# Attention scores of two layers as three float32r products of split queries and keys

## The chip, the cores and the metric

The kernel runs on one core of a Trainium2 chip. The metric is the device time of one execution in microseconds; the median of several runs is compared. A profiled execution is the source of every row below. TensorE is called PE, its weight loads PEld, VectorE DVE, ScalarE ACT, GpSimd POOL, and SyncE SP.

## What is computed

The reference is a network of three blocks over 512 positions of 1024 channels: one block with stick-breaking attention and an MLP, and then two layers of a second type. The change touches the attention of the second type only, which the reference writes so (cut):

```python
c_kv = _rmsnorm(p[..., o1:o2], g_kv[l])                  # 256 channels
kv = (c_kv @ w_ukv[l]).reshape(b, s, 8, 64 + 64)         # k_nope and v of 8 heads
k_rope = _apply_rope(p[..., o2:o3], cos, sin)            # 32 channels, shared by the heads
sc = q_nope . k_nope + q_rope . k_rope                   # 512 x 512 a head
p = softmax(sc / sqrt(96)); o = p @ v
```

Beside it, in the same layer, a depthwise convolution of 31 taps over 512 channels and a layer norm are computed; both results go into the output projection `w_o`.

## The kernel before, in words

All activations lie with channels on the 128 partitions and the 512 positions along the free dimension. Every big product is made of three float32r products: a tile is split into a high half (`whi`, `xh`, ...: the value cast to float32r) and a low half (the rest), and `mm3` (L505) adds high x high, high x low and low x high into one PSUM bank (L507, L508, L509). Weights are loaded by SP, cast by ACT (L421) and their low halves subtracted on POOL (L422), up to three units ahead of their use.

`layer2` runs once for each of the two layers. In it come, in the order of the code: four tiles of gated units (`glu`); the shared rotary key `pk` (L1165 to L1178); the key/value input, two tiles, and the query input, three tiles (`low_rank`, L1184), each split as soon as it is made, so the key/value input is split without its norm's factor; that factor, `rkv`, is computed inside the first query tile's products (L1210) and the query's factor inside the gate projection that follows (L1213). Since the key/value input is unscaled, the value tiles `v` are multiplied by a column of the factor (`col`, made by `column`, L675, with eight tiny products a layer), and the keys by its row (L1310).

The attention goes over four pairs of heads (L1306). For each pair: one projection makes the keys of both heads, the query projection of each head goes to a PSUM bank of the name `mm`, and DVE multiplies it into the tile `q` (L1315). `attend` (L1271) makes for each of four blocks of queries one score product of float32 tiles (L1275), which is two records of PE in the profile; then DVE's row maximum (L1277), ACT's Exp, and the scaling by the sum's reciprocal, on POOL for the first block and on ACT for the others (L1283). The probabilities are transposed on PE (L1292), split by ACT and DVE (`ph`, `pl`), and multiplied by `v` into the bank `av`. PE works between these on the projections of the next heads and on the output projection (`y_part`).

The convolution's taps fill the other engines: those of DVE are one instruction (L1347), those of POOL an ACT product `pd` and a POOL sum `cacc` (L1361, L1363), four `pd` buffers in turn. A list, `pace`, says behind which ACT instruction each `pd` is issued. The order on each engine is otherwise set by the framework's scheduler when the program is built.

Of the kernel before, what the change touches and what calls it, by code (L numbers as in the profile page):

```python
# [13 lines left out]
F32 = mybir.dt.float32  # L14
FR = mybir.dt.float32r
I32 = mybir.dt.int32
AF = mybir.ActivationFunctionType
ALU = mybir.AluOpType
# [3 lines left out]
P = 128  # L22
S = 512
# [42 lines left out]
PACE_GLU, PACE_ROPE, PACE_RANK, PACE_HEAD = 4, 1, 2, 2  # L66
# [223 lines left out]
class Kern:  # L290
# [274 lines left out]
            ready = cs  # L565


    def split(self, pool, src, tags, scale=None, lo_eng=None):

        hi, lo = (pool.tile([P, S], FR, name=t) for t in tags)  # L570
        self.split_into(hi, lo, src, scale, lo_eng)
        return hi, lo

# [543 lines left out]
    def layer2(self, l, carry=None):  # L1117
        tc, nc = self.tc, self.nc
        mm = nc.tensor.matmul
        V, A, G = nc.vector, nc.scalar, nc.gpsimd  # L1120
# [6 lines left out]
        pp = pa_.__enter__()  # L1127
# [14 lines left out]
        lp = lp_.__enter__()  # L1142
# [3 lines left out]
        pace = []  # L1146

        def glu(pa, pg):
            V.tensor_tensor(out=pg, in0=pg, in1=r, op=ALU.mult)
            V.tensor_tensor(out=pa, in0=pa, in1=r, op=ALU.mult)  # L1150
            u = lp.tile([P, S], F32, name="u", bufs=NCV)
            sig = self.act(AF.Sigmoid, out=u, in_=pg)
            if us:
                pace.extend([sig] * PACE_GLU)
            V.tensor_tensor(out=u, in0=u, in1=pa, op=ALU.mult)
            us.append(u)
# [8 lines left out]
        pk = self.proj(pp, "b", acts)  # L1165
        tkr = lp.tile([P, S], F32, name="tmp", bufs=3)
# [3 lines left out]
        kt = {}  # L1170
        for b in range(2):
            for e in range(2):
                kt[e, b] = lp.tile([P, S], F32, name=f"k{e}{b}")
            if b == 0:
                V.tensor_tensor(out=kt[1, b][0:64], in0=pk[0:64], in1=tkr[0:64], op=ALU.add)
            else:
                A.copy(out=kt[1, b][0:64], in_=kt[1, 0][0:64])
            A.copy(out=kt[0, b][64:128], in_=kt[1, 0][0:64])  # L1178


        r2 = lp.tile([P, S], F32, name="tmp", bufs=3)
        A.activation(out=r2, in_=r, func=AF.Square)

        def low_rank(n, gname, tag, between=None):  # L1184
            out = []
            acc = self.new_acc()
            part = pp.tile([P, S], F32, name="b")
            for j in range(n):
                ps = self.proj(pp, "b", acts, between if j == 0 else None)
                if j == 0:  # L1190
                    A.activation(out=part, in_=ps, func=AF.Square)
                else:
                    V.tensor_tensor(out=part if j < n - 1 else acc, in0=part, in1=self.square(ps), op=ALU.add)
                out.append(self.split(lp, ps, (f"{tag}h{j}", f"{tag}l{j}"), scale=self.v(gname, l, j)))
                pace.extend([self.last_hi] * PACE_RANK)
            return out, acc

        def low_rank_scale(acc, n, dst=None):

            tot, _ = self.total(pp, "b", acc)  # L1200
            w = self.new_acc()
            V.tensor_tensor(out=tot, in0=tot, in1=r2, op=ALU.mult)
            self.rsqrt(w, tot, n * P, tot)
            dst = tot if dst is None else dst
            V.tensor_tensor(out=dst, in0=tot, in1=r, op=ALU.mult)
            return dst

        ckv, acckv = low_rank(2, "g_kv_2", "kv")
        rkv = lp.tile([P, S], F32, name="rho")
        cq, accq = low_rank(3, "g_q_2", "cq", lambda: low_rank_scale(acckv, 2, rkv))  # L1210
        rhos = []

        def q_norm():  # L1213
            rhos.append(self.column(lp, pp, "b", rkv))
            rhos.append(low_rank_scale(accq, 3))

        for i in range(GLU_EARLY, 4):
# [1 line left out]
            self.proj(pp, "b", acts, q_norm if i == GLU_EARLY else None, pa)  # L1219
            self.proj(pp, "b", acts, None, pg)  # L1220
            glu(pa, pg)
        col, rq = rhos
        tq = []
        for e in range(2):
            x = lp.tile([P, S], F32, name=f"tq{e}")
# [15 lines left out]
        def bank(name):  # L1241
            turns[name].rotate(-1)
            return turns[name][0].tile([P, S], F32, name=name)
# [16 lines left out]
        for t in range(4):  # L1260
                vt = lp.tile([P, H2, P], FR, name="v", bufs=4)
                src = vps[t].rearrange("p (h d) -> p h d", d=64)
                A.activation(out=vt[:, :, 0:64], in_=src, func=AF.Identity, scale=col[:, t : t + 1], bias=0.0)
                ins = V.scalar_tensor_tensor(out=vt[:, :, 64:P], in0=src, scalar=col[:, t : t + 1], in1=vt[:, :, 0:64].bitcast(F32), op0=ALU.mult, op1=ALU.subtract)
                vst.append(vt)
        gate.append(ins)

# [3 lines left out]
        def attend(h, q, k, y):  # L1271
            probs = []
            for qb in range(4):
                s = bank("s")
                mm(s, lhsT=q[:, qb * P : (qb + 1) * P], rhs=k, start=True, stop=True)  # L1275
                nm = lp.tile([P, 1], F32, name="nm", bufs=4)
                V.tensor_reduce(out=nm, in_=s, axis=AX.X, op=ALU.max, negate=True)  # L1277
                pr = yp.tile([P, S], F32, name="ul" if h % 2 else "uh")
                sm = lp.tile([P, 1], F32, name="sm", bufs=4)
                ins = self.act(AF.Exp, out=pr, in_=s, bias=nm, accum_out=sm)  # L1280
                V.reciprocal(out=sm, in_=sm)
                if qb >= POOL_BLOCKS:
                    A.activation(out=pr, in_=pr, func=AF.Identity, scale=sm, bias=0.0)  # L1283
                else:
                    G.tensor_tensor(out=pr, in0=pr, in1=sm.broadcast_to((P, S)), op=ALU.mult)
                probs.append(pr)
            pace.extend([ins] * PACE_HEAD + [None] * POOL_TAPS)
            av = bank("av")
            for t in range(4):
                pt = bank("t")  # L1290
                for qb in range(4):
                    nc.tensor.transpose(pt[:, qb * P : (qb + 1) * P], probs[qb][:, t * P : (t + 1) * P], self.ident)  # L1292
                ph = lp.tile([P, S], FR, name="ph", bufs=2)
                pl = lp.tile([P, S], FR, name="pl", bufs=2)
                A.copy(out=ph, in_=pt)
                V.tensor_tensor(out=pl, in0=pt, in1=ph.bitcast(F32), op=ALU.subtract)
                mm(av, lhsT=vst[t][:, h, :], rhs=ph, start=t == 0, stop=False)
                mm(av, lhsT=vst[t][:, h, :], rhs=pl, start=False, stop=t == 3)
            e = h % 2
            me, other = slice(64 * e, 64 * e + 64), slice(64 - 64 * e, 128 - 64 * e)  # L1300
            t = lp.tile([P, S], F32, name="tmp", bufs=3)
            A.copy(out=t[me], in_=av[other])
            V.tensor_tensor(out=y[me], in0=av[me], in1=t[me], op=ALU.add)

        yacts = []
        for p in range(4):  # L1306
            pk = self.proj(pmm, "mm", ckv)
            for e in range(2):
                me = slice(64 * e, 64 * e + 64)
                V.tensor_tensor(out=kt[e, p % 2][me], in0=pk[me], in1=rkv[me], op=ALU.mult)  # L1310
            y = lp.tile([P, S], F32, name="tmp", bufs=3)
            for e in range(2):
                pq = self.proj(pmm, "mm", cq)
                q = lp.tile([P, S], F32, name="q", bufs=2)
                ins = V.tensor_tensor(out=q, in0=pq, in1=tq[e], op=ALU.mult)  # L1315
                gate.append(ins)
                attend(2 * p + e, q, kt[e, p % 2], y)
            yacts.append(self.split(yp, y, ("yh", "yl")))

        ypss = [pmm.tile([P, S], F32, name="mm") for _ in range(2)]  # L1320
# [83 lines left out]
        for i in range(KT):  # L1404
            ps = ypss[i] if i < NYB else self.proj(pmm, "mm", yacts + uacts)
# [7 lines left out]
        pp = pp_.__enter__()  # L1413
# [46 lines left out]
        with tc.manual_schedule(engines={mybir.EngineType.PE}):  # L1460
            for c, ks in enumerate(chunks2()):
# [70 lines left out]
                for m in range(KT - tail):  # L1532
                    ps = ds[m] if m < NDOWN else self.proj(pp, "b", a)
# [140 lines left out]
```

## Time and profile before

| | us |
|---|---|
| median of 3 runs | 1873.52 (1872.75 to 1874.34) |
| profiled execution, whole | 1875.88 |
| its span, first to last instruction | 1874.2 |
| PE busy in the span | 1821.1 |
| DVE, ACT, POOL busy | 1020.8, 1041.2, 1128.6 |

The profiled execution's own time is 1.68 us longer than its span and 2.36 us longer than the median. Busy time says that an engine has something in work; two instructions of PE overlap, so the step from start to start tells their price, not the duration.

### The profile page before, as it was taken

Reading aid. Unit: us, or ns where it says so; the run is one execution under the profiler, and the core shown is the slowest. Engines: PE = TensorE matmul, PEld = TensorE weight load, DVE = VectorE, ACT = ScalarE, POOL = GpSimd, SP = SyncE. Lnnn points to the kernel's source line nnn. Section 1 sums busy time; section 2 is a strip of 40 time slices with the busy share of each in tenths; the row PEclk is TensorE's granted clock in tenths of the full one; section 3 lists DMA queues with packets and bytes.
Section 4 is the critical chain, followed back from the end, with each engine's and each line's share of the span. In section 5 each row is a group of like instructions: output and inputs, shape, how many; then the busy total and the mean of one; then the engine's idle time right before and its main releaser. Section 6 shows DMA issues by size and latency. Waiting matters only on the chain. (4 is left out here: it accounts for less than half of the span.)

```text
span 1874.2 us, 25701 instructions
## 1 busy us (share of the span) xinstructions
PE 1821.1 (97%) x9726; PEld 1530.7 (82%) x9726; DVE 1020.8 (54%) x1524; ACT 1041.2 (56%) x1630; POOL 1128.6 (60%) x618
## 2 busy tenths in 40 slices
PE   8999999999999999999998999999999998999997
PEld 6877888888888888766778998998866788898996
DVE  5665553725022017898596252553899498253454
ACT  6666643633233236788556373663779566364563
POOL 5233454654554556866577695875866467585872
PEclk9999999999999999999998999999999999999999
DMA  5113386276987852300346595862210214353551
GB/s 188 68 57 107 136 229 199 95 220 177 288 220 223 239 160 79 100 30 23 141 124 214 163 296 168 253 178 83 89 60 23 105 59 136 114 190 135 162 165 45
DMA packets 96092, 268.95 MB, mean 144 GB/s; under 512 B 9824, under 2 KB 11872, under 8 KB 95328
## 3 DMA queue, kind: packets, MB, share of 16 engines
q1 hardware_dynamic: 73376, 188.66, 29.6%
q0 software_dynamic: 19072, 37.75, 11.4%
q10 hardware_dynamic: 3520, 40.90, 5.7%
q8 instruction: 76, 1.25, 0.3%
q14 instruction: 48, 0.39, 0.1%
HBM read 265.18 MB, written 77.59 MB: 183 GB/s over the span
## 5 line engine op out<-in xcount | busy, mean ns | idle before, releaser
L422 POOL TENSOR_TENSOR wlo<-raw,whi 128x1024 fp32r<-128x1024 f32 (+1 forms) x354 | 857.1, 2436 | 609.4 <-ACT whi L421 559.9
L421 ACT CAST whi<-raw 128x1024 fp32r<-128x1024 f32 (+1 forms) x356 | 369.8, 1041 | 470.9 <-PE b L508 343.6
L507 PE MATMUL b<-xh,whi 128*128 128x512 f32 (+1 forms) x720 | 274.1, 381 | 2.7 <-ACT xh L580 2.7
L508 PE MATMUL b<-xl,whi 128*128 128x512 f32 (+1 forms) x720 | 270.4, 376 | 3.5 <-DVE xl L581 3.5
L509 PE MATMUL b<-xh,wlo 128*128 128x512 f32 (+1 forms) x720 | 269.7, 375 | 0.0
L507 PE MATMUL b<-ah,whi 128*128 128x512 f32 (+1 forms) x640 | 242.7, 379 | 0.0
L509 PE MATMUL b<-ah,wlo 128*128 128x512 f32 (+1 forms) x640 | 242.3, 379 | 0.0
L508 PE MATMUL b<-al,whi 128*128 128x512 f32 (+1 forms) x640 | 242.3, 379 | 0.0
L508 PEld LDWEIGHTS b<-xl,whi 128*128 128x128 f32 x720 | 136.2, 189 | 32.4 <-DVE xl L581 4.5
L507 PEld LDWEIGHTS b<-xh,whi 128*128 128x128 f32 x720 | 136.3, 189 | 30.9 <-ACT xh L580 3.1
L509 PEld LDWEIGHTS b<-xh,wlo 128*128 128x128 f32 x720 | 136.2, 189 | 26.1
L509 PEld LDWEIGHTS b<-ah,wlo 128*128 128x128 f32 x640 | 120.4, 188 | 22.3
L507 PEld LDWEIGHTS b<-ah,whi 128*128 128x128 f32 x640 | 120.4, 188 | 22.0
L508 PEld LDWEIGHTS b<-al,whi 128*128 128x128 f32 x640 | 120.4, 188 | 22.0
L1363 POOL TENSOR_TENSOR cacc<-cacc,pd 128x510 f32<-128x510 f32 (+14 forms) x94 | 119.6, 1273 | 26.6 <-ACT pd L1361 22.9
L1347 DVE SCALAR_TENSOR_TENSOR cv<-u,vec,cv 128x497 f32<-128x497 f32 (+13 forms) x146 | 108.2, 741 | 8.5 <-ACT cv L1337 6.6
L1480 DVE TENSOR_TENSOR b<-b,snap 128x256 f32<-128x256 f32 x108 | 46.3, 429 | 83.6 <-PE b L509 82.5
L1534 DVE TENSOR_TENSOR x<-x,b 128x512 f32<-128x512 f32 x46 | 31.5, 688 | 103.6 <-PE b L509 103.6
L1006 DVE TENSOR_TENSOR b<-rl,b 128x512 f32<-128x512 f32 x32 | 22.1, 696 | 96.9 <-ACT rl L1005 96.9
L507 PE MATMUL mm<-xh,whi 128*128 128x512 f32 x176 | 70.8, 402 | 0.0
L508 PE MATMUL mm<-xl,whi 128*128 128x512 f32 x176 | 70.2, 399 | 0.0
L509 PE MATMUL mm<-xh,wlo 128*128 128x512 f32 x176 | 70.1, 398 | 0.0
(502 smaller groups left out, 4434.3 us busy)
## 6 DMA issues: line engine op xcount, KB each, us to landing
raw<-w SPq DMA_DIRECT2D x215, 512.0 KB, 3.6
raw<-S SPq DMA_DIRECT2D x144, 256.0 KB, 2.9
S<-wq POOLq DMA_DIRECT2D x32, 1024.0 KB, 13.0
raw<-wq SPq DMA_DIRECT2D x108, 256.0 KB, 2.9
raw<-w SPq DMA_DIRECT2D x23, 256.0 KB, 2.9
S<-wq POOLq DMA_DIRECT2D x8, 512.0 KB, 8.6
x<-xT SPq DMA_DIRECT2D x8, 256.0 KB, 6.3
S<-wq ACTq DMA_DIRECT2D x4, 512.0 KB, 4.6
```

The source lines that it names most:

```text
L421: cast = nc.scalar.copy(out=hi[:, cs], in_=raw[:, cs])
L422: rest = (eng or nc.gpsimd).tensor_tensor(out=lo[:, cs], in0=raw[:, cs], in1=hi[:, cs].bitcast(F32), op=ALU.subtract)
L507: mm(ps, lhsT=wb[0], rhs=xb[0], start=start, stop=False, **kw)
L508: mm(ps, lhsT=wb[0], rhs=xb[1], start=False, stop=False, **kw)
L509: mm(ps, lhsT=wb[1], rhs=xb[0], start=False, stop=stop, **kw)
L1006: V.tensor_tensor(out=ps, in0=rl, in1=ps, op=ALU.mult)
L1347: ins = V.scalar_tensor_tensor(out=acc[:, o], in0=us[i][:, u], scalar=self.v("w_dw_conv_2", l, i * CONV_K + k), in1=acc[:, o], op0=ALU.mul ...
L1363: G.tensor_tensor(out=acc[:, o], in0=acc[:, o], in1=pd, op=ALU.add)
L1480: V.tensor_tensor(out=out, in0=a, in1=b, op=ALU.add)
L1534: V.tensor_tensor(out=self.x[m], in0=self.x[m], in1=ps, op=ALU.add)
```

## The change

The scores become three float32r products. For that, the query tile is split: ACT casts its high half, POOL subtracts the low half. The keys are split too: ACT casts the projection's rows into a high tile, DVE subtracts the low one (in place of the multiplication by the factor's row), and the rotary rows of all four key tiles are copied as high and low halves. The key/value input is now multiplied by its factor before it is split, so the splits come behind the norm's factor; the value tiles are then copied and subtracted without a column, and the column's tiny products go.

```diff
-            if b == 0:
-                V.tensor_tensor(out=kt[1, b][0:64], in0=pk[0:64], in1=tkr[0:64], op=ALU.add)
-            else:
-                A.copy(out=kt[1, b][0:64], in_=kt[1, 0][0:64])
-            A.copy(out=kt[0, b][64:128], in_=kt[1, 0][0:64])
+                kt[e, b] = tuple(lp.tile([P, S], FR, name=f"k{part}{e}{b}") for part in "hl")
+        V.tensor_tensor(out=pk[0:64], in0=pk[0:64], in1=tkr[0:64], op=ALU.add)
+        kr, kl = pk[0:64], kt[1, 0][1][0:64]
+        A.copy(out=kt[1, 0][0][0:64], in_=kr)
+        V.tensor_tensor(out=kl, in0=kr, in1=kt[1, 0][0][0:64].bitcast(F32), op=ALU.subtract)
+        for e, b, rows in ((0, 0, slice(64, 128)), (0, 1, slice(64, 128)), (1, 1, slice(0, 64))):
+            A.copy(out=kt[e, b][0][rows], in_=kr)
+            A.copy(out=kt[e, b][1][rows], in_=kl.bitcast(F32))
...
-        cq, accq = low_rank(3, "g_q_2", "cq", lambda: low_rank_scale(acckv, 2, rkv))
+        def kv_norm():
+            low_rank_scale(acckv, 2, rkv)
+            for j, ps in enumerate(kvs):
+                V.tensor_tensor(out=ps, in0=ps, in1=rkv, op=ALU.mult)
+                ckv.append(low_split(ps, "g_kv_2", "kv", j))
+
+        cq, accq = low_rank(3, "g_q_2", "cq", kv_norm)
...
-            rhos.append(self.column(lp, pp, "b", rkv))
...
-                A.activation(out=vt[:, :, 0:64], in_=src, func=AF.Identity, scale=col[:, t : t + 1], bias=0.0)
-                ins = V.scalar_tensor_tensor(out=vt[:, :, 64:P], in0=src, scalar=col[:, t : t + 1], in1=vt[:, :, 0:64].bitcast(F32), op0=ALU.mult, op1=ALU.subtract)
+                A.copy(out=vt[:, :, 0:64], in_=src)
+                ins = V.tensor_tensor(out=vt[:, :, 64:P], in0=src, in1=vt[:, :, 0:64].bitcast(F32), op=ALU.subtract)
...
-                mm(s, lhsT=q[:, qb * P : (qb + 1) * P], rhs=k, start=True, stop=True)
+                self.mm3(s, [t[:, qb * P : (qb + 1) * P] for t in q], k, True, True)
...
-                V.tensor_tensor(out=kt[e, p % 2][me], in0=pk[me], in1=rkv[me], op=ALU.mult)
+                hi, lo = (t[me] for t in kt[e, p % 2])
+                A.copy(out=hi, in_=pk[me])
+                V.tensor_tensor(out=lo, in0=pk[me], in1=hi.bitcast(F32), op=ALU.subtract)
...
-                attend(2 * p + e, q, kt[e, p % 2], y)
+                attend(2 * p + e, self.split(lp, q, ("qh", "ql"), lo_eng=G, bufs=2), kt[e, p % 2], y)
```

The scheduler's order changes with it, from the rotary key to the layer norm of the convolution in each layer, and nowhere else; SP's queue keeps its order.

On PE, at the first scores of the first layer, the order before was this (`s` is the score's bank, `k` the keys, `cqh` and `cql` the query input's halves, `mm` the bank of a projection):

```order
L508 MATMUL mm<-cql_6308,whi 128x512
L1275 MATMUL s<-k_6137,q 128x512 x2
L509 MATMUL mm<-cqh_6307,wlo 128x512
L507 MATMUL mm<-cqh_6345,whi 128x512
L508 MATMUL mm<-cql_6346,whi 128x512
```

and now it is this:

```order
L508 MATMUL mm<-cql_6319,whi 128x512
L509 MATMUL mm<-cqh_6318,wlo 128x512
L507 MATMUL s<-kh_6137,qh 128x512
L508 MATMUL s<-kl_6138,qh 128x512
L507 MATMUL s<-kh_6137,qh 128x512
L509 MATMUL s<-kh_6137,ql 128x512
L508 MATMUL s<-kl_6138,qh 128x512
L509 MATMUL s<-kh_6137,ql 128x512
L507 MATMUL mm<-cqh_6356,whi 128x512
```

Two float32 scores became six products, of which the fourth is the first that reads the query's low half.

On ACT, at the same place, behind the casts of the value tiles `v` (`uh` is a tile of probabilities), the order before was this:

```order
L1263 ACTIVATE v<-s,col 128x8x64
L421 CAST whi<-raw 128x1024
L390 ACTIVATE uh,sm<-s,nm 128x512 x2
L421 CAST whi<-raw 128x1024
L1283 ACTIVATE uh<-uh,sm 128x512
```

and now it is this:

```order
L1276 CAST v<-s 128x8x64
L421 CAST whi<-raw 128x1024
L1324 CAST kh_6137<-mm 64x512
L1324 CAST kh_6139<-mm 64x512
L577 CAST qh<-q 128x512
L421 CAST whi<-raw 128x1024
L390 ACTIVATE uh,sm<-s,nm 128x512 x2
L577 CAST qh<-q 128x512
L1296 ACTIVATE uh<-uh,sm 128x512
L1324 CAST kh_6141<-mm 64x512
```

Three casts and the second weight cast stand ahead of the first Exp now, and further ones come between the Exps.

On POOL, at the same place, the order before was this:

```order
L1363 TENSOR_TENSOR cacc<-cacc,pd 128x510
L1363 TENSOR_TENSOR cacc<-cacc,pd 128x511
L422 TENSOR_TENSOR wlo<-raw,whi 128x1024
L1285 TENSOR_TENSOR uh<-uh,sm 128x512
L422 TENSOR_TENSOR wlo<-raw,whi 128x1024
```

and now it is this:

```order
L1378 TENSOR_TENSOR cacc<-cacc,pd 128x511
L422 TENSOR_TENSOR wlo<-raw,whi 128x1024
L578 TENSOR_TENSOR ql<-q,qh 128x512
L422 TENSOR_TENSOR wlo<-raw,whi 128x1024
L1298 TENSOR_TENSOR uh<-uh,sm 128x512
L578 TENSOR_TENSOR ql<-q,qh 128x512
```

The first query's low half stands between two subtractions of weights, ahead of the first scaling.

## Rows read from the trace of the kernel before

**Rows 1.** The page: span, then each engine's busy us, share and instructions.

```profile
span 1874.2 us, 25701 instructions
PE 1821.1 (97%) x9726; PEld 1530.7 (82%) x9726; DVE 1020.8 (54%) x1524; ACT 1041.2 (56%) x1630; POOL 1128.6 (60%) x618
```

**Rows 2.** Windows: stretch, us, busy us of PE, PEld, DVE, ACT, POOL; clock, DMA.

```profile
804.10:883.10 79.00, 77.13 (x337) 51.34 (x337) 72.16 (x141) 71.16 (x148) 51.55 (x41) 1.00 0.07 26
...
1379.90:1458.90 79.00, 77.11 (x338) 51.31 (x336) 72.21 (x141) 71.22 (x148) 51.67 (x41) 1.00 0.07 26
...
852.00:862.00 10.00, 10.00 (x46) 6.73 (x45) 9.48 (x19) 9.95 (x21) 9.76 (x8) 1.00 0.00 0
```

**Rows 3.** PE's timeline, 871 to 896 us: start, us, what.

```profile
871.00 1.88 PE L1275 MATMUL s<-k,q 128*128 128x512 f32 x4
872.72 0.38 PE L1292 MATMUL t<-ident,uh 128*128 128x128 f32 x2
...
893.00 0.40 PE L507 MATMUL mm<-yh,whi 128*128 128x512 f32 x1
...
895.10 0.39 PE L507 MATMUL t<-yh,whi 128*128 128x512 f32 x1
```

**Rows 4.** PE's timeline, 781 to 892 us; in brackets idle time and its releaser.

```profile
781.57 0.95 PE L679 MATMUL b<-e,rho 128*128 128x1 f32 x8
782.38 1.10 PE L609 MATMUL b<-acc,ones 128*128 128x512 f32 x2
...
790.31 0.39 PE L1255 MATMUL mm<-whi,kvh 128*128 128x512 f32 x1
...
800.69 0.47 PE L507 MATMUL mm<-cqh,whi 128*128 128x512 f32 x1 [1.03 <-DVE k L1310]
...
802.11 1.99 PE L1275 MATMUL s<-k,q 128*128 128x512 f32 x4
...
891.22 1.02 PE L609 MATMUL cv<-u,ones 128*128 128x512 f32 x2
```

**Rows 5.** DVE's timeline, 772 to 888 us.

```profile
772.05 0.69 DVE L1205 TENSOR_TENSOR rho<-b,r 128x512 f32<-128x512 f32 x1
...
799.17 1.38 DVE L1310 TENSOR_TENSOR k<-mm,rho 64x512 f32<-64x512 f32 x2
...
801.36 0.69 DVE L1315 TENSOR_TENSOR q<-mm,tq 128x512 f32<-128x512 f32 x1
...
887.02 0.69 DVE L1382 TENSOR_TENSOR u<-cacc,cv 128x512 f32<-128x512 f32 x1 [1.37 <-POOL cacc L1363]
```

**Rows 6.** ACT's timeline, 797 to 890 us.

```profile
797.90 1.05 ACT L421 CAST whi<-raw 128x1024 fp32r<-128x1024 f32 x1
804.13 0.69 ACT L390 ACTIVATE uh<-s,nm 128x512 f32<-128x512 f32 x1 [5.18 <-DVE nm L1277]
...
851.61 1.07 ACT L1295 CAST ph<-t 128x512 fp32r<-128x512 f32 x2
852.57 0.71 ACT L390 ACTIVATE ul<-s,nm 128x512 f32<-128x512 f32 x1
...
886.76 1.07 ACT L1295 CAST ph<-t 128x512 fp32r<-128x512 f32 x2 [1.93 <-PE t L1292]
889.70 0.58 ACT L1302 COPY tmp<-av 64x512 f32<-64x512 f32 x1 [1.87 <-PE av L1298]
```

**Rows 7.** POOL's timeline, 796 to 811 us.

```profile
796.75 2.66 POOL L1363 TENSOR_TENSOR cacc<-cacc,pd 128x510 f32<-128x510 f32 x2
799.37 2.38 POOL L422 TENSOR_TENSOR wlo<-raw,whi 128x1024 fp32r<-128x1024 f32 x1
805.63 1.04 POOL L1285 TENSOR_TENSOR uh<-uh,sm 128x512 f32<-128x512 f32 x1 [3.88 <-DVE sm L1281]
...
810.49 1.28 POOL L1363 TENSOR_TENSOR cacc<-cacc,pd 128x509 f32<-128x509 f32 x1 [1.47 <-ACT pd L1361]
```

**Rows 8.** Waits in 797 to 892 us: total us, times, longest.

```profile
ACT uh L390 <- DVE nm L1277: 6.0, 3, 5.2
```

More of the change, by code (lines that the diff above doesn't have):

```diff
@@ L565, in proj_halves, with split @@
             ready = cs
-    def split(self, pool, src, tags, scale=None, lo_eng=None):
-        hi, lo = (pool.tile([P, S], FR, name=t) for t in tags)
+    def split(self, pool, src, tags, scale=None, lo_eng=None, **kw):
+        hi, lo = (pool.tile([P, S], FR, name=t, **kw) for t in tags)
         self.split_into(hi, lo, src, scale, lo_eng)
@@ L1172, in layer2, with low_rank @@
             for e in range(2):
-                kt[e, b] = lp.tile([P, S], F32, name=f"k{e}{b}")
-            if b == 0:
-                V.tensor_tensor(out=kt[1, b][0:64], in0=pk[0:64], in1=tkr[0:64], op=ALU.add)
-            else:
-                A.copy(out=kt[1, b][0:64], in_=kt[1, 0][0:64])
-            A.copy(out=kt[0, b][64:128], in_=kt[1, 0][0:64])
+                kt[e, b] = tuple(lp.tile([P, S], FR, name=f"k{part}{e}{b}") for part in "hl")
[6 more added lines that the diff above has]
+            A.copy(out=kt[e, b][1][rows], in_=kl.bitcast(F32))
         r2 = lp.tile([P, S], F32, name="tmp", bufs=3)
         A.activation(out=r2, in_=r, func=AF.Square)
-        def low_rank(n, gname, tag, between=None):
+        def low_rank(n, gname, tag, between=None, split=True):
             out = []
@@ L1193, in low_rank, with low_split @@
                     V.tensor_tensor(out=part if j < n - 1 else acc, in0=part, in1=self.square(ps), op=ALU.add)
-                out.append(self.split(lp, ps, (f"{tag}h{j}", f"{tag}l{j}"), scale=self.v(gname, l, j)))
-                pace.extend([self.last_hi] * PACE_RANK)
+                out.append(low_split(ps, gname, tag, j) if split else ps)
             return out, acc
+        def low_split(ps, gname, tag, j):
+            parts = self.split(lp, ps, (f"{tag}h{j}", f"{tag}l{j}"), scale=self.v(gname, l, j))
+            pace.extend([self.last_hi] * PACE_RANK)
+            return parts
         def low_rank_scale(acc, n, dst=None):
@@ L1206, in low_rank_scale @@
             return dst
-        ckv, acckv = low_rank(2, "g_kv_2", "kv")
+        kvs, acckv = low_rank(2, "g_kv_2", "kv", split=False)
         rkv = lp.tile([P, S], F32, name="rho")
-        cq, accq = low_rank(3, "g_q_2", "cq", lambda: low_rank_scale(acckv, 2, rkv))
+        ckv = []
+        def kv_norm():
[4 more added lines that the diff above has]
+        cq, accq = low_rank(3, "g_q_2", "cq", kv_norm)
         rhos = []
         def q_norm():
-            rhos.append(self.column(lp, pp, "b", rkv))
             rhos.append(low_rank_scale(accq, 3))
@@ L1221, in layer2 @@
             glu(pa, pg)
-        col, rq = rhos
+        rq, = rhos
         tq = []
```

## The prediction

> **What bounds the kernel now.** I read the page first: PE is busy for 97% of the span, ACT, DVE and POOL for 54 to 60% [rows 1]. Such a share is an average over stages, so next came the windows of the stage that the change touches, layer by layer. From the first Exp of the attention to the last scaling of a probability tile (804.1 to 883.1 us, and the same 79.0 us in the second layer) PE is busy for 77.1 us, but ACT for 71.2 and DVE for 72.2 [rows 2]. In 852 to 862 us ACT has 0.05 us of 10 free. So the stage is PE's by a narrow margin: 7.8 us of ACT and 6.8 us of DVE are free in it.
>
> Then PE's timeline, for pitches instead of durations (durations overlap). Four records of a float32 score product, which are two scores, start at 871.00 and the next instruction at 872.72: 0.86 us a score [rows 3]. In a run of float32r products the one at 893.00 and the ninth after it, at 895.10, give 0.233 us each [rows 3]. Three of them are 0.70 us.
>
> **The scores on PE.** 64 scores, 32 a layer, each 0.16 us cheaper: -5.1 us a layer, -10.3 us in all, if PE sets the pace.
>
> The Trainium skill speaks of this price: in "FP8 and Floating Point Precision", section TensorE Precision Notes, it says that a true FP32 product takes four passes through the array. Four of the measured 0.233 us would be 0.93 us a score and a saving of 0.23 us, 14.9 us in all; the trace has 0.86 us, and the trace decides.
>
> **The column products.** Eight records at 781.57 us that turned the key/value scale into columns go; the next product starts at 782.38 [rows 4]: 0.8 us a layer. What follows them waits for DVE anyway: the second query projection stands 1.03 us for the key tiles and the first score comes when q is there [rows 4]. I take nothing; bounds 0 and -0.8 us a layer.
>
> **Scaling the key/value input before its split.** Four DVE products of 128x512 (0.6 us pitch) are added, and the splits move behind the scale. The scale is ready at 772.7 us [rows 5]; two products, a cast and a subtraction later, at about 775, both halves stand, and their first reader on PE comes at 790.31 [rows 4]. Two PSUM banks are held until then; by the rotation of seven banks the next taker is the gate projection, which starts 18 products ahead of 781.57, at 777.4. So this is hidden, with 2.4 us to spare; without that cover every further us counts in full. Behind the splits' casts on ACT stand ten taps of the convolution, which go to POOL. POOL, which takes 1.28 us for each sum, then does them in one piece up to about 801 us, when it would have finished at 799.4 anyway [rows 7].
>
> **The start of the attention.** Before: DVE makes both key tiles from 799.17, frees the bank at 800.5, and q follows at 801.36 [rows 5]. Now ACT first casts the weights (797.90 to 798.9 [rows 6]), then two key halves (some 0.5 us each), DVE subtracts twice with a tap between, and q comes after that: bank free at about 801.9, q at 802.5, its high half at 803.1, its low half on POOL (behind a weight subtraction of 2.4 us, then 1.04 us [rows 7]) at 804.2. PE has the first two scores done at 804.95 instead of 803.8, but three products of the projection are still to come that were behind it before: 0.8 us late in PE's work, and the first Exp, which came at 804.13, comes at about 805.4: 1.3 us late.
>
> **The steady stage.** On DVE the key product becomes a key subtraction of the same shape (0.68 us), and one tap fewer is left: 71.5 us to do. On POOL eight subtractions of 1.04 us join 51.6 us of work in 79: room enough. On ACT 16 casts a layer are new: 8 key halves of 64x512 from PSUM, like the 64x512 copy of 0.58 us, and 8 query halves of 128x512, like the ph casts, of which two take 0.96 us from start to next start [rows 6]; I take 0.50 us for each. Three stand ahead of the first Exp; 13 x 0.50 = 6.5 us lie in the stage, and one weight cast of 1.0 us moves ahead of it. ACT then has 71.2 + 6.5 - 1.0 = 76.7 us to do, and with 805.4 for its first Exp it is through with the scalings at 882.1 + m, where m is what it idles on the way. Before: 883.1. After the scalings stand transposes, casts and the last products, a chain whose waits (1.93 and 1.87 us) no change touches [rows 6], so the end moves with it.
>
> PE alone would allow more: 0.8 us late at the start, 30 scores of 0.16 us saved: 4.0 us a layer earlier. It cannot have it, since ACT stands in its way: ACT's gain is 1.0 - m us a layer.
>
> m is 7.8 us now, while ACT isn't the bound; in the saturated 852 to 862 us it is at a rate of 0.4 us for 79 [rows 2]. These are the bounds: +0.6 to -6.8 us a layer. A loaded engine has work queued, so I am nearer to the lower one, but the waits in which ACT stands for a row maximum of DVE (6.0 us over the first layer's attention, 5.2 of it ahead of the first Exp) or for a transpose do not all go [rows 6, 8]: m = 1.5 us. Per layer +0.5 us, for two layers +1.0 us.
>
> **What is hidden.** The convolution's last tap sum ends on POOL just ahead of 887.02, and the fourth of its norm's products on PE starts at 891.22 [rows 4, 5]: over 3 us of room, more than the stage shrinks in my forecast. Behind the attention nothing moves.
>
> **The sum.** The profiled execution took 1875.88 us, 2.36 above the median of 1873.52. 1875.9 + 1.0 = 1876.9; on the scale of the median 1874.5 us. A difference of 0.2% (3.7 us) is about what a measurement of this kernel can tell from none.
>
> **The rivals.**
>
> *PE stays the bound.* If ACT's busy time holds slack that the rows don't show (of the timeline's pitches in 852 to 862 us, I count 9.65 us of work where the window shows 9.95 [rows 2]; over a stage 2 to 3 us), ACT ends 3 us earlier than reckoned and PE sets the pace. Then 4.0 us a layer are kept: 1865.5 us; half-way 1869. For it speaks that PE waits seldom now, since projections are done ahead as filler; against it 90% of DVE and ACT in the stage.
>
> *The chain grows longer: slower.* Each head's query now goes DVE, ACT, POOL and then PE, where it went DVE, PE. PE takes its queue in order, so the third product of a score waits for POOL, and behind it stand transposes and value products for which ACT and DVE wait in turn. If ACT keeps the idle time it has, m = 7.8: 6.8 us a layer lost, 1887 us; at half of it (m = 3.9) 2.9 a layer, 1879.3. It decides against me from m = 2.9. For it: POOL's instructions are long (2.4 us for weights, 1.28 for taps), and the low half stands behind them; against it: a projection stands one head ahead in the queue.
>
> *The splits ahead of the attention come late.* If the gate projection waits for the banks, 2.4 us of margin must be gone first; I give it no chance of its own and put it with the slower case.
>
> **Chances.** ACT takes over and eats the gain, within 0.2%: 0.38 (own range 1872 to 1877.2, from m = 0.4 to 2.9). PE stays the bound, fully or in good part, faster: 0.34. Longer chain, slower: 0.28. The likeliest is the first, 1874.5. A range for 8 in 10 must reach into both others: 1865.5, the PE bound with nothing more, leaves out little below; above, 1882 leaves out the upper part of the longer chain.
>
> **What would show it.** In the profile after: PE's three products of a score at 0.70 us; PE busy less than now in the attention, with idle time released by ACT (ph, uh, ul) or DVE (pl), where it is some 2 us a layer now; ACT at 95% or more between the first Exp and the last scaling, and this stretch 75 to 79 us long. If instead PE is at 97% there and the stretch 74, the first rival is right. If PE's waits name ql (POOL), and ACT is still under 92%, the second. What would make the whole reckoning wrong is a wait that stands ahead of the attention: a gate projection that starts later after 777 us, or a first Exp later than 1.3 us.

## The result, and the profile after

The changed kernel takes 1891.52 us (median of 4 runs, 1889.05 to 1892.79), against 1873.14 us for the kernel before beside it: ratio 1.0097, interval 1.0084 to 1.0109, some 18 us slower. I had predicted 1874.5 us, at most 1882. The profiled execution took 1889.05 us. The lines of its page that answer to [rows 1]:

```profile
span 1887.3 us, 25846 instructions
PE 1814.5 (96%) x9774; PEld 1534.9 (81%) x9774; DVE 1026.5 (54%) x1528; ACT 1061.2 (56%) x1670; POOL 1148.7 (61%) x634
```

PE is busy for 6.6 us less than before (5.2 of them outside the stretches of the table below, where the change leaves the program as it is) and the span is 13 us longer, so PE stands. (The two profiled executions lie 2.7 us above and 2.5 us below the medians of 1873.14 and 1891.52; hence 13 and not 18.) From the list of its waits over the whole span (us, times, longest):

```profile
...
PE t L1268 <- DVE tq L1243: 8.0, 1, 8.0
...
PE s L1268 <- ACT u L390: 3.7, 1, 3.7
...
PE s L507 <- ACT uh L390: 3.0, 4, 1.2
...
PE mm L507 <- DVE kl L1325: 1.8, 2, 0.9
```

The first two are in the value products, ahead of the attention: the 8.0 us in the second layer, the 3.7 us in the first. To see what each step of a layer lost, I took four times in each layer from the timelines, with the start of DVE's product of the rotated key (`b<-b,tk`, L1167) as zero: the first value cast on ACT, the first Exp, the length from there to the end of the last probability scaling, and the length from there to the first addition to `x`. Two numbers in a cell are the two layers. The rows below the second are the experiments.

| kernel | ratio, 95% interval | first value cast | first Exp | first Exp to last scaling | to `x` |
|---|---|---|---|---|---|
| before | 1 | 45.8 / 46.7 | 54.3 / 55.3 | 79.1 / 79.1 | 40.5 / 40.5 |
| after | 1.0097, 1.0084-1.0109 | 49.3 / 53.9 | 60.4 / 65.4 | 79.5 / 79.5 | 41.1 / 41.0 |
| e1 | 1.0090, 1.0075-1.0105 | 50.1 / 50.6 | 61.6 / 62.1 | 79.5 / 79.5 | 41.1 / 41.0 |
| e2 | 1.0020, 1.0011-1.0030 | 45.4 / 51.4 | 58.7 / 60.8 | 76.3 / 76.4 | 40.5 / 40.5 |
| e3 | 1.0053, 1.0038-1.0068 | 44.7 / 50.0 | 55.8 / 61.5 | 79.4 / 79.5 | 41.1 / 41.1 |
| e4 | 1.0060, 1.0045-1.0075 | 44.9 / 50.0 | 57.3 / 61.5 | 79.5 / 79.5 | 41.1 / 41.0 |
| e5 | 1.0066, 1.0054-1.0079 | 49.3 / 50.0 | 61.4 / 62.0 | 79.5 / 79.5 | 41.1 / 41.1 |
| e6 | 1.0028, 1.0018-1.0037 | 44.8 / 45.9 | 55.9 / 56.9 | 79.5 / 79.4 | 41.1 / 41.1 |
| e7 | 1.0029, 1.0018-1.0040 | 44.8 / 45.9 | 56.8 / 57.9 | 79.5 / 79.5 | 41.0 / 41.1 |
| e8 | 1.0015, 1.0006-1.0024 | 45.4 / 46.4 | 58.9 / 59.4 | 76.4 / 76.4 | 40.5 / 40.5 |
| e9 | 1.0059, 1.0046-1.0072 | 45.5 / 46.4 | 54.5 / 55.4 | 78.1 / 78.1 | 46.0 / 47.0 |
| e10 | 1.0034, 1.0022-1.0047 | 44.9 / 45.9 | 56.9 / 57.9 | 79.0 / 79.0 | 41.3 / 41.3 |
| e11 | 1.0084, 1.0070-1.0098 | 44.8 / 45.9 | 55.1 / 57.0 | 79.6 / 80.8 | 45.5 / 46.4 |
| e12 | 1.0073, 1.0059-1.0086 | 44.8 / 45.9 | 55.5 / 56.6 | 80.2 / 80.2 | 45.2 / 46.5 |
| e13 | 1.0006, 0.9997-1.0015 | 45.4 / 45.9 | 57.4 / 56.9 | 77.7 / 77.7 | 40.6 / 40.6 |
| e14 | 1.0096, 1.0082-1.0110 | 44.9 / 45.9 | 55.1 / 55.7 | 74.8 / 74.9 | 51.6 / 51.9 |
| e15 | 1.0154, 1.0140-1.0168 | 44.9 / 45.9 | 56.4 / 57.4 | 75.2 / 75.2 | 56.4 / 56.5 |
| e16 | 0.9969, 0.9956-0.9981 | 44.7 / 45.9 | 53.7 / 54.8 | 76.4 / 76.4 | 40.5 / 40.5 |

The sum of a row is the time of the whole stretch: before 173.9 / 174.8, after 180.9 / 186.0. The two layers lose 7.0 and 11.2 us, together the 18 us that the medians show. Of that, 3.5 and 7.2 us are lost up to the first value cast, 2.6 and 3.0 from there to the first Exp, 0.4 to 0.5 in the stage and 0.6 behind it. (The rest of the program, which the change leaves as it is, took 5 us less in this profiled execution than in the one before.)

**What stands ahead of the value cast.** ACT's timeline of the second layer, from the key/value casts to the query norm:

```profile
1355.51 1.27 ACT L580 ACTIVATE kvh<-b,vec 128x512 fp32r<-128x512 f32 x2
1356.66 1.94 ACT L1376 ACTIVATE pd<-u,vec 128x508 f32<-128x508 f32 x3
...
1360.49 2.53 ACT L1376 ACTIVATE pd<-u,vec 128x502 f32<-128x502 f32 x4
1365.70 0.71 ACT L1376 ACTIVATE pd<-u,vec 128x500 f32<-128x500 f32 x1 [2.68 <-POOL cacc L1378]
1367.04 0.72 ACT L1376 ACTIVATE pd<-u,vec 128x502 f32<-128x502 f32 x1 [0.63 <-POOL cacc L1378]
1368.38 0.72 ACT L1376 ACTIVATE pd<-u,vec 128x504 f32<-128x504 f32 x1 [0.61 <-POOL cacc L1378]
1369.00 0.67 ACT L390 ACTIVATE acc<-b,epst 128x512 f32<-128x512 f32 x1
```

The logarithm of the query norm, last line, stands behind ten taps that are tied to the casts of the key/value and query inputs. The taps write into four `pd` buffers, and POOL empties one in 1.28 us, so ACT stands 3.9 us and the norm with it. DVE's timeline has what feeds the logarithm (the first line) and what hangs from it, down to the last `tq`:

```profile
1363.54 0.69 DVE L1208 TENSOR_TENSOR b<-b,tmp 128x512 f32<-128x512 f32 x1
...
1371.26 0.70 DVE L618 SCALAR_TENSOR_TENSOR b<-b,acc 128x512 f32<-128x512 f32 x1 [4.35 <-ACT acc L390]
...
1378.21 0.68 DVE L1243 TENSOR_TENSOR tq<-te,b 64x512 f32<-64x512 f32 x1
```

POOL's timeline shows why taps pile up; it had nothing to do before them:

```profile
1347.88 2.40 POOL L422 TENSOR_TENSOR wlo<-raw,whi 128x1024 fp32r<-128x1024 f32 x1 [4.04 <-ACT whi L421]
1355.69 2.42 POOL L422 TENSOR_TENSOR wlo<-raw,whi 128x1024 fp32r<-128x1024 f32 x1 [5.41 <-ACT whi L421]
1358.07 4.02 POOL L1378 TENSOR_TENSOR cacc<-cacc,pd 128x508 f32<-128x508 f32 x3
1362.05 2.39 POOL L422 TENSOR_TENSOR wlo<-raw,whi 128x1024 fp32r<-128x1024 f32 x1
1364.38 9.29 POOL L1378 TENSOR_TENSOR cacc<-cacc,pd 128x502 f32<-128x502 f32 x7
```

PE's timeline then shows the wait, and that it costs more than its length:

```profile
1370.52 0.39 PE L1270 MATMUL mm<-whi,kvl 128*128 128x512 f32 x1
1378.94 0.80 PE L1268 MATMUL t<-whi,kvh 128*128 128x512 f32 x1 [8.04 <-DVE tq L1243]
1379.54 0.63 PE L1269 MATMUL t<-wlo,kvh 128*128 128x512 f32 x1
1379.96 0.63 PE L1270 MATMUL t<-whi,kvl 128*128 128x512 f32 x1
```

The second group of value products waits for `tq`, which it does not read. It waits for the bank: `tq` is the last reader of the query norm's bank. That bank is new here. As the built programs have it, the value products take banks 5, 2, 3 and 7 in both kernels; the query norm's bank was 6 before and is 4 (first layer) or 2 (second) now, the gate tile's was 4 or 2 and is 7. The column products had taken a bank of the seven in turn, the key/value tiles now hold two of them longer, and so later tiles lie elsewhere.

### The profile page after: what moved, and what is told of

It is laid out like the page before. It is cut to its first block, busy times and chain, and to the rows that moved or that the text cites. A ratio compares the mean times of both kernels' runs of the same rounds, so it can differ in the third digit from the quotient of the medians.

```text
span 1887.3 us, 25846 instructions
## 1 busy us (share of the span) xinstructions
PE 1814.5 (96%) x9774; PEld 1534.9 (81%) x9774; DVE 1026.5 (54%) x1528; ACT 1061.2 (56%) x1670; POOL 1148.7 (61%) x634
## 5 line engine op out<-in xcount | busy, mean ns | idle before, releaser
L581 DVE SCALAR_TENSOR_TENSOR xl<-x,vec,xh 128x256 fp32r<-128x256 f32 (+1 forms) x56 | 66.2, 1194 | 6.7 <-ACT xh L580 6.6
```

The lines of the kernel that those rows point to most:

```text
L581: nc.vector.scalar_tensor_tensor(out=lo, in0=src, scalar=scale, in1=hi.bitcast(F32), op0=ALU.mult, op1=ALU.subtract)
```

## The experiments

The kernel before ran at 1873 to 1878 us on the chips used, so ratios are compared.

**Which part: e1 and e2.** e1 is the changed kernel without the scaling (`ckv, acckv = low_rank(2, "g_kv_2", "kv")`, and `kv_norm` only makes `rkv`); keys and values stay unscaled, the column products stay out. e2 is the kernel before with the scaling ahead of the split; `k` becomes a copy.

> The changed kernel with the key/value input split where it was split before, unscaled; the scaling of keys and values by the key/value norm is left out, and the column products too. So it holds the score part of the change alone. Theory A (taps): the loss ahead of the attention comes from the taps that are tied to the late key/value casts; they pile up behind POOL, ACT stands with its four product buffers full, and the query norm's logarithm stands behind them. Then PE's two waits of 3.7 us (for the gate tile u) and 8.0 us (for tq) go, and the time is 1891.5 - 11.7 = about 1880, the first Exp some 2 us late in a layer. Rival B (score side): the longer way of keys and queries over ACT and POOL, with three more key copies ahead, makes the first Exp late: 1888 to 1892, the two waits stay.

> The kernel before with the other part alone: scores stay float32 products, the key/value input is scaled ahead of its split, the column products go, and the key product on DVE becomes a copy of the same shape. Theory A: the waits ahead of the attention come with this part, 1873.1 + 11.7 = about 1885, and PE waits for u or tq in front of the value products. Rival B: 1873 +- 3, since the part is hidden as forecast.

e1 1.0090, e2 1.0020: against theory A, as far as it put the loss with the scaling. In e2, too, taps stand ahead of the query norm's logarithm behind the late casts, but there ACT waits only 1.15 us for POOL (second layer) and the logarithm comes 0.5 to 0.6 us later than in the kernel before; with both parts in, it is 4.1 to 4.4 us later. So the pile-up takes both parts, or the order that the scheduler makes of them. But the score part was not guilty in the way of rival B either. The waits of e1 in PE's view:

```profile
PE mm L1264 <- ACT pd L1372: 9.4, 2, 4.7
```

4.7 us in each layer stand ahead of the first value product, and the query norm's logarithm comes sooner than in the kernel before. In e1's program the query norm's bank is 5, which is the first that the value products take. (The view names a tap's product `pd` of ACT. In the second layer the last read of the bank, by `tq`, ends at 1381.47 us, and the value product starts at 1381.62; e7, which moves the banks alone, ends the wait.) Without the column products, banks move in e1 too, and it was no clean test of the score part. That gave theory C.

**Taps: e3 and e4.** In e3 the four taps of a layer stand behind the squares of the two tiles, in e4 behind the query norm. The edit of e3 (cut):

```
+                if not split:
+                    pace.extend([sq] * PACE_RANK)
...
-            pace.extend([self.last_hi] * PACE_RANK)
+            if tag != "kv":
+                pace.extend([self.last_hi] * PACE_RANK)
```

> The changed kernel, with the four taps a layer that were placed behind the two key/value casts placed behind the squares of the same tiles, where those casts stood before. Nothing is left out. Theory A: POOL has work again while the scale is made, ACT doesn't run into full buffers ahead of the query norm, about 1880. Rival B, or a third (the four products and the late halves themselves hold up PE): 1888 to 1892.

> The changed kernel, with the same four taps placed behind the query norm's last ACT step instead, later than in the changed kernel. Nothing is left out. If theory A's mechanism is the order on ACT (the query norm behind taps that wait for a product buffer), the norm comes earlier by 3 to 5 us and the time falls to 1880 to 1885, though POOL gets its work later still. If what costs is the time that POOL stood idle (some 9 us ahead of the key/value casts in the second layer) and the convolution ends late by it, the time stays at 1890 or grows.

1.0053 and 1.0060, 7 to 8 us of the 18 back. The value cast comes 4.4 to 4.5 us sooner in the first layer and 3.9 in the second, with either. That e4 gains nearly as much, though POOL gets the taps later still, says that what cost was the order on ACT, with the norm behind taps that wait for a buffer, and not POOL's idle time. The second layer keeps a wait of 3.9 us for `tq` in both, with a norm that now comes sooner than in the kernel before.

**Banks: e5 to e8.** e5 is the changed kernel with another order of banks, e6 adds the early taps, e7 is e1 and e8 is e2 with banks that suit them.

```
-BANKS = (("av", 1), ("t", 2), ("mm", 1), ("mm", 1), ("s", 1), ("s", 1))
+BANKS = (("t", 1), ("mm", 1), ("mm", 1), ("s", 1), ("t", 1), ("av", 1), ("s", 1))   # e5, e6, e8
+BANKS = (("mm", 1), ("t", 2), ("mm", 1), ("s", 1), ("av", 1), ("s", 1))             # e7
```

> The changed kernel with the banks of the attention laid out in another order, nothing else. In the built programs the last bank of the gate tile is 7 and that of the query norm 4 (first layer) or 2 (second); the value products take banks 5, 2, 3, 7. Here they take 3, 5, 1, 7. Theory C (banks): the change shifted which freed bank a value product meets; PE's wait of 8.0 us for tq in the second layer goes down to the 3.7 us of the gate bank, as in the first: 4 us less, a ratio of 1.0075 after 1.0097. Theory A (taps alone) has the late query norm as the cause, whatever the bank: 1.0097.

> The taps of the experiment with early taps (ratio 1.0053) and the bank order together. Theory C: the 3.9 us for tq that was left in the second layer goes as well, both layers lose only what lies behind the value products: the first Exp some 3 us late after them and 1 us in the rest, 4 us a layer, ratio about 1.003 to 1.004. If banks don't matter: 1.0053.

> The score part alone (key/value scale left out, ratio 1.009) with a bank order in which the value products don't meet the query norm's bank: there it was 5, the first one that they take. Theory C: PE's two waits of 4.7 us go, 1.009 - 0.005 = 1.004; what is left is the score part's own price, 4 us a layer. If the score part itself holds the attention up ahead of the value products, 1.009 stays.

> The scaling ahead of the split alone, with float32 scores (ratio 1.002), with the same bank order as the first of these. Theory C: PE's waits of 4.2 us (first layer) and 4.5 us (second) go. If the attention stage keeps its 76.3 us a layer (79.1 in the kernel before), the time is 8.7 us less: ratio 0.9975, faster than the kernel before. If the stage was short only because DVE and POOL did taps during those waits, it goes back to 79 and the ratio is 1.000. If banks don't matter: 1.002.

e5 took 4.0 us off the second layer's value cast. In e6 the value cast is 0.9 us sooner than before the change in both layers. The two value-product waits are gone from PE's list. e7 took 5.3 and 4.7 us off e1's. Theory C holds. In e6 1.0028 is left, 5 us, for the whole change; e7, the score part alone, has 1.0029. That is the score part's price beside the kernel before; on top of the scaling it is higher, as e16 will show. e8 missed: the second layer's wait for `tq` went, but the 4.2 us of the first layer are no bank of the query norm. There PE stands at the query projection for the value subtraction, which DVE does only after seven taps, and now it did so in both layers.

**The scaling alone, put right: e9 and e16.** e9 is e8 with `TAP_GATES = (38, 46)`, which lets five taps fewer stand ahead of the value subtraction. e16 is e8 with the early taps of e3.

> The scaling ahead of the split alone, with the bank order (ratio 1.0015), and with five taps fewer on DVE ahead of the value subtractions (the first gate at tap 38 instead of 43). There DVE did seven taps, 5.45 us, ahead of the first value subtraction, and PE stood 4.2 us a layer for the bank that it frees. Theory: those waits go, 8.4 us less, ratio 0.997 to 0.999, faster than the kernel before. Rival: the five taps, 0.65 us each, make DVE the bound in the attention stage (72.2 + 3.3 us of 76.4) and take most of it back: 1.000 to 1.0015.

> The scaling ahead of the split alone, with float32 scores, early taps and the bank order: DVE then has two taps ahead of the first value subtraction, as in the kernel before, instead of seven. PE's wait of 4.2 us a layer for that subtraction goes, and the convolution is not put off. Theory: the query norm comes 0.9 us sooner than in the kernel before, the rest is as there, 1 to 2 us a layer less: ratio 0.998 to 0.9995. Rival: one more wait takes its place, 1.0015.

e9 missed: the waits went and the first Exp came 4.0 to 4.5 us sooner than in e8, but the five taps were late at the other end. Counted from the first Exp, the convolution's sum came 2.8 us later than in the kernel before, and the stretch to `x` grew by 5.5 to 6.5 us. e16 has two taps ahead of the subtraction, as before; POOL's share begins early in it. It is 0.9969, faster than both kernels. PE is full in its stage, where it had 1.9 us free [rows 2]:

```profile
1375.06:1451.45 76.39, 76.37 (x337) 50.62 (x335) 71.88 (x140) 70.97 (x148) 50.98 (x41) 1.00 0.08 26
```

The 1.8 us a layer for which PE waited for `uh` of POOL in the kernel before are not among e16's waits, and 0.8 us less of PE's work lies in the stage. The stage is as short in e2 and e8, so this comes with the scaling and not with the banks or the early taps; no run has those two on the kernel before alone.

e16 is also e6 without the score part: same scaling, taps and banks, float32 scores. So on this base the score part, the three products with their splits, costs 1.0028 against 0.9969, some 11 us, and not 5: from e16 to e6 a layer's first Exp comes 2.1 to 2.2 us later, the stage takes 3.1 us more and what follows 0.6.

**What sets the stage: e10 to e15,** all on e6. e10: `POOL_BLOCKS = 2`. e11: `V.tensor_copy(out=hi, in_=pk[me])` for the keys' high half. e12: the weight cast behind the first two Exps. e13: one of the three scalings on ACT left out of each head. e14: `(q[0], q[0])` for the two query halves, so the low half counts for nothing. e15: the product with the keys' low half left out.

> The changed kernel with early taps and the bank order (ratio 1.0028), and two instead of one of the four probability scalings of a head on POOL: ACT has 8 x 0.61 = 4.9 us a layer less to do, POOL 8 x 1.04 = 8.3 more. If ACT sets the attention stage (76.7 us of work in 79.5), it becomes 3 to 4 us a layer shorter: ratio 0.999 to 1.000. If it is the length of the chain over POOL and not ACT's load, it becomes no shorter or longer: 1.003 or more.

> The same base (ratio 1.0028), with the high half of the keys written by DVE instead of ACT: ACT has 8 x 0.5 = 4 us a layer less, DVE as much more (70.5 to 74.6), and the two engines don't wait for each other at the first keys. If ACT's load is the bound: 2 to 3 us a layer in the stage and about 1 us at the first Exp, ratio 0.9985 to 0.9995. If DVE is as near to the bound as ACT is: 1.002 to 1.003.

> The same base (ratio 1.0028), with the weight cast that ACT did just ahead of the first Exp put behind the first two Exps, where the kernel before has it. The cast waited 2.9 us for PE and let the first Exp come 1.25 us after its row maximum. If that wait counts in full: 1.2 us a layer less, ratio 1.0015. If ACT's queue only takes it back later (the same work is to do in the stage): 1.0028.

> The changed kernel with early taps and the bank order (ratio 1.0028, its stage from the first Exp to the last scaling 79.4 us), and the scaling of one of the three probability tiles that ACT scales in each head left out: ACT has 8 x 0.61 = 4.9 us a layer less to do, and nothing goes to another engine. If ACT's load sets the stage (76.7 busy of 79.4), it becomes 3.5 to 4.5 us shorter, down to PE's 74.6 and a little: 75 to 76, ratio 0.999. If the way of a head from engine to engine sets it (moving the same 4.9 us to POOL brought 0.45 us), it stays above 78.5.

> The same base, with the third product of each score taking the high half of the queries in place of the low half: as many products, but none that waits for POOL (the low half is still made, and not used). If PE's queue, held up by the low half from POOL, sets the stage, it becomes shorter by 1.5 us or more. If ACT's load does, it stays at 79.4 +- 0.4, and the first Exp comes 0.3 us sooner at most.

> The same base with two products for a score instead of three: the one with the low half of the keys is left out, 32 x 0.233 = 7.5 us a layer less for PE. If PE still sets the pace in the stage, it becomes 5 us shorter or more. If ACT does, it stays within 0.7 us of 79.4, and only what lies ahead of the first Exp gains some 0.5 us.

Only e13 is plain to read. 4.4 us less of ACT's work (76.7 to 72.3 us in the stage) made the stage 1.8 us shorter and what follows 0.4: half of it, between the two outcomes expected.

```profile
1384.71:1462.37 77.66, 72.84 (x359) 54.28 (x358) 69.39 (x136) 72.29 (x151) 60.10 (x49) 1.00 0.08 25
```

No engine is full there. In e10 the same work went to POOL, and the whole gained nothing. In e11, e12, e14 and e15 the last column tells what happened: the order of the queues is set anew when a kernel is built, more taps fell behind the attention, and the convolution ended last. In e14 the stage is 4.6 us shorter than in e6, but 10 of POOL's tap sums stand behind it instead of 2. The second layer's scalings end at 1464.7 us, and POOL sums taps for 16.7 us more:

```profile
1472.10 3.97 POOL L1382 TENSOR_TENSOR cacc<-cacc,pd 128x508 f32<-128x508 f32 x3
1476.03 1.04 POOL L1378 TENSOR_TENSOR pd<-u,vec 128x510 f32<-128x510 f32 x1
1477.02 4.37 POOL L1382 TENSOR_TENSOR cacc<-cacc,pd 128x511 f32<-128x511 f32 x3
1481.34 4.66 POOL L422 TENSOR_TENSOR wlo<-raw,whi 128x1024 fp32r<-128x1024 f32 x2
```

PE then waits 4.2 us a layer for the split convolution output. So e14 and e15 do not tell the price of the low half or of PE's products by themselves; in these orders neither edit brought anything, 7.5 us a layer less for PE (e15) included.

## Why the prediction was wrong

**The step that failed: "So this is hidden, with 2.4 us to spare."** I looked at two covers, PE's banks while the tiles wait for their scale, and POOL's finish. The first held: PE has no wait at the gate projection. The second was the wrong question. I knew that ten taps would go "in one piece" and asked when POOL would be through, not what stands behind the taps on ACT. There it is the query norm, and from it hang the gate tile, `tq` and with them two banks. e3 and e4 show it with 3.9 to 4.5 us a layer. I had named the place ("the splits ahead of the attention come late"), but with a bank wait that did not come, and gave it no chance of its own. In e2 the norm's logarithm is only 0.5 to 0.6 us late: without the score part this cover nearly held, and what e2 loses comes from a bank and from taps on DVE. Nor had I anything for what the scaling gains: in e2, e8 and e16 the stage takes 2.7 us less than before.

**The second: "I take nothing" for the column products.** Their 0.8 us of PE's time was not the point. They also took a bank, and I counted instructions and not allocations. e5 and e6 show 4.0 us in the second layer for where the query norm's bank lies, e7 about 5 us a layer.

**The start of the attention, +1.3 us.** With taps and banks put right (e6) the first Exp is 1.6 us late in both layers; without that, 6.0 and 10.2. The nearness of 1.6 to 1.3 is luck: in e6 the value cast comes 0.9 us sooner than before, and from there the first Exp takes 11.0 us instead of 8.5. So the mechanism was right, and the term measured 2.5 us, about twice what I gave it. In e6 PE stands 2.1 us a layer for the second key's low half, where it stood 1.03 us for the key tiles [rows 4]. ACT's timeline of the second layer of the changed kernel:

```profile
1386.91 0.58 ACT L1324 CAST kh<-mm 64x512 fp32r<-64x512 f32 x1
1388.24 0.58 ACT L1324 CAST kh<-mm 64x512 fp32r<-64x512 f32 x1 [0.75 <-DVE kl L1325]
1390.35 0.63 ACT L577 CAST qh<-q 128x512 fp32r<-128x512 f32 x1 [1.53 <-DVE q L1330]
1393.86 1.05 ACT L421 CAST whi<-raw 128x1024 fp32r<-128x1024 f32 x1 [2.88 <-PE mm L508]
1394.94 0.69 ACT L390 ACTIVATE uh<-s,nm 128x512 f32<-128x512 f32 x1
```

The three casts are those I priced. The fourth, a second weight cast, I had counted as 1.0 us that leaves the stage, and not as something that the first Exp stands behind; it waits 2.9 us for PE. e12 put it behind; the first Exp came only 0.3 us sooner and the kernel became slower, so moving it bought nothing.

**The scores on PE: right, and worth nothing here.** The price is as forecast, three products at 0.233 us:

```profile
1400.32 0.39 PE L507 MATMUL s<-kh,qh 128*128 128x512 f32 x1
1400.55 0.40 PE L508 MATMUL s<-kl,qh 128*128 128x512 f32 x1
1400.79 0.39 PE L509 MATMUL s<-kh,ql 128*128 128x512 f32 x1
1401.02 0.40 PE L507 MATMUL s<-kh,qh 128*128 128x512 f32 x1
```

PE's busy time in the stage fell from 77.1 to 74.6 us (30 scores at 0.16 us would make 4.8 of it; the rest is not accounted for), ACT's rose from 71.2 to 76.8, where I had reckoned 76.7. The windows of the two stages:

```profile
808.24:887.74 79.50, 74.61 (x362) 54.44 (x360) 70.53 (x137) 76.78 (x160) 59.60 (x48) 1.00 0.07 24
1394.94:1474.47 79.53, 74.59 (x362) 54.43 (x360) 70.58 (x137) 76.80 (x160) 59.60 (x48) 1.00 0.07 24
```

**m, the idle time of ACT in the stage,** was 79.5 - 76.8 = 2.7 us, where I took 1.5 and had 2.9 as the point at which the slower rival begins. A mis-sized term: 1.2 us a layer. e13 says that even this is not ACT's load alone. The signs that I had named are there otherwise: ACT is busy for 97% of the stage, and PE's waits in it name ACT for the greater part. In e6, whose stage is the same, the longest in the second layer are:

```profile
PE s L507 <- ACT uh L390: 1.5, 2, 1.2
PE t L1309 <- POOL uh L1302: 1.0, 1, 1.0
PE mm L508 <- DVE yl L578: 0.7, 1, 0.7
```

None of its waits there names the queries' low half `ql`, by which I would have known the rival with the longer chain. What else holds the stage is open: no run took the chain over POOL apart without setting the queues anew.

**"Over 3 us of room" for the convolution, and "Behind the attention nothing moves".** The first was a misreading, and the second fell with it. I had compared the sum with the fourth of the norm's products, which reads it. But the first of them waits as well: it writes the one bank of the tiles `cv`, and the addition that ends the sum is the last to read that bank. Before the change there were 0.25 us between the two (887.02 + 0.69 [rows 5] and this line):

```profile
887.96 1.02 PE L609 MATMUL cv<-u,ones 128*128 128x512 f32 x2
```

In the changed kernel the addition ends 1.1 us later, counted from the first Exp, and PE stands 0.76 us for it in each layer; the last value products behind it come later, and ACT's copy waits 2.69 us for them instead of 1.87 [rows 6]:

```profile
892.95 1.12 PE L609 MATMUL cv<-u,ones 128*128 128x512 f32 x2 [0.76 <-DVE u L1397]
...
894.81 0.58 ACT L1315 COPY tmp<-av 64x512 f32<-64x512 f32 x1 [2.69 <-PE av L1311]
```

That is the 0.6 us a layer behind the attention. In e16 PE does not stand there, and the stretch has its 40.5 us again. e9, e11, e12, e14 and e15 put the sum off by 2.8 to 9.2 us.

**The sum.** Against my +0.5 us a layer (1.3 at the first Exp, 0.8 back in the stage), the layers lost 7.0 and 11.2. The miss is 4.7 and 8.9 us at the first Exp, 1.2 and 1.3 in the stage, 0.6 and 0.6 behind it: 17.3 us, of which 13.6 are the first Exp's, by e6 nearly all taps and banks. The rival with the longer chain (1887 us) came nearest in time, but not by its mechanism: m stayed below its point. The rival in which PE stays the bound had nothing for it: PE is busy for 94% of the stage.

## What to carry to other kernels

When an edit delays an instruction, list what the queue does behind it up to the next thing that another engine waits for, and count the buffers between the two: the loss here was an in-order engine standing on four full buffers. An edit that drops an allocation from a rotating pool can move the later tiles to other banks; compare the banks of the first tiles of the next stage with the last readers of the stage before it. A part that looks guilty may only stand wrong: the scaling costs 1.0020 as first placed and gives 0.9969 when taps and banks follow it, while the scores, which carried the expected gain, lose 5 us even with banks that suit them (e7), and 11 us on top of the scaling put right (e6 against e16).

## What the runs showed of the hardware

Two waits of PE were each followed by a slow stretch. The windows of the changed kernel (us, then PE's busy time first; the granted clock is the third number from the end):

```profile
793.43:794.90 1.47, 1.47 (x6) 1.24 (x7) 1.47 (x3) 1.46 (x2) 1.47 (x2) 1.00 0.20 31
794.95:798.30 3.35, 3.35 (x9) 2.65 (x8) 2.81 (x5) 3.35 (x7) 3.27 (x3) 0.50 0.67 253
...
1378.94:1381.60 2.66, 2.66 (x6) 2.15 (x7) 0.61 (x1) 0.61 (x1) 2.50 (x3) 0.50 0.58 200
1381.67:1384.00 2.33, 2.33 (x11) 1.91 (x10) 0.00 (x0) 0.57 (x1) 1.84 (x2) 0.93 0.00 0
```

After the wait of 8.0 us the clock is at 0.50, its lower level of 1.2 GHz, for 2.7 us, and products come 0.43 us apart instead of 0.233. After the wait of 3.7 us six products run at full clock, and then the clock is at 0.50 for 3.4 us. By an estimate, six and eight products at 0.43 instead of 0.233 us, some 1.2 and 1.6 us come on top of the waits, which my price of a wait did not have. The Trainium skill says in "TensorE: Matmul & The Clock Gate", section "HAM oscillation — how this bites in real kernels", that a wait of the engine throttles it and that what follows starts at the low clock. The trace agrees after the wait of 8.0 us, with the 0.50 above; after the wait of 3.7 us the clock fell only six products later.
